# A decoder layer on one core: modulation weights on two of three parts of the first contraction, the final norm's weight ahead of r, and a turned order in the branches

## The chip, the cores and the metric

The kernel runs on one core of a Trainium2 chip. A core has TensorE (PE, matrix products into PSUM), VectorE (DVE), ScalarE (ACT), GpSimd (POOL), SyncE (SP, which here only issues DMAs) and 16 DMA engines that all queues share. The engines run on their own and wait for one another through semaphores; each takes its instructions in order. The metric is the device time of one execution in microseconds (us), lower is better.

## What is computed

One decoder layer on a sequence of 256 tokens of width 1024, in float32. A conditioning vector c gives nine modulation vectors, mod = silu(c) @ ada_w + ada_b; ada_w is 1024 x 9216, 36 MiB, and is read once.

```python
c_act = jax.nn.silu(c)
mod = c_act @ ada_w[l] + ada_b[l]
sh1, sc1, g1, sh2, sc2, g2, sh3, sc3, g3 = jnp.split(mod, N_MOD, axis=-1)
u = modulate(rms_norm(h, norm_ffn1_w[l]), sh1, sc1)
h = h + FFN_RESIDUAL_WEIGHT * g1[:, None, :] * swiglu(u, ffn1_w_in[l], ffn1_w_out[l])
u = modulate(rms_norm(h, norm_mix_w[l]), sh2, sc2)
h = h + g2[:, None, :] * hybrid_mixer(u, positions, mix_w_in[l], ...)
u = modulate(rms_norm(h, norm_ffn2_w[l]), sh3, sc3)
h = h + FFN_RESIDUAL_WEIGHT * g3[:, None, :] * swiglu(u, ffn2_w_in[l], ffn2_w_out[l])
return rms_norm(h, norm_final_w)
```

`rms_norm(x, w)` is x / sqrt(mean(x^2) + 1e-6) * w, `modulate(x, shift, scale)` is x * (1 + scale) + shift. `swiglu` multiplies by w_in (1024 x 5632), takes silu(gate) * up and multiplies by w_out (2816 x 1024). The mixer is one wide product u @ mix_w_in, an SSD (state space) branch and a retention branch, each multiplied by a matrix of 2048 x 1024, gated, added and multiplied by mix_w_out.

## The kernel before

Activations lie transposed: 128 features on the partitions, 256 tokens along the row, eight such tiles for the width of 1024. Every large product is made of three matmuls per pair of tiles (`mm3`): weights and activations are each split into a high half, rounded to the matmul's type (fp32r), and a low half, the remainder. high x high, high x low and low x high are added up in PSUM. For the weights the high half is a cast on ACT (`half`, L137), the low half a subtraction on DVE (L138). A group of 24 matmuls (8 row tiles x 3) fills one column tile of 128. `mm3` has a `turned` form that takes a triple in the order low x high, high x high, high x low, and `contract` and `pair_project` use it for the fifth of eight triples.

**Weights** come in tiles of 128 x 2048 floats (1 MiB; 768 KiB for a last part of six row tiles) from four staging buffers (tag wst, `STAGE_BUFS`), loaded on SP by `load`, split by `half` in two steps of 128 x 1024 into four high and four low buffers (`HALF_BUFS`). A staging buffer is free again when DVE has done the second low half.

**Modulation** is computed in the gaps. `ada_piece` (through `ada_next`) takes one quarter of one of the nine vectors: it loads 1 MiB of ada_w into a staging buffer on SP, and DVE forms two dot products of 128 x 1024 with the activated c (`ada_dots`, L195). After a vector's fourth quarter its bias is added (L207). `ada_todo` lists the pieces in the order of vectors 2, 4, 3, 5, 7, 6, 8; `ada_next(3, 5)` takes the next only if it belongs to vector 3 or 5.

**The first contraction**, `contract("ffn1_w_out", 22, ...)`, goes over four pairs of column tiles (f2). For each it loads three parts of 8, 8 and 6 row tiles (k0), splits, multiplies both column tiles, and after each part calls `each()`, here `ada_next(3, 5)`. With the eight pieces of vectors 3 and 5 left at its start, the first eight of its twelve parts take one each, and the last four none. After a pair's last part `residual`'s `done` updates h, squares it for the next norm and splits the new activations. Then `modulated` runs: `early_project` multiplies by the first two tiles of mix_w_in before the norm's factor is known, while DVE and ACT work it out (`rstd`) and apply it (L265, L236, L237); the dt projection (L590, L591) is the first to need the result.

Which instruction comes when is set by a planner that orders each engine's instructions from the program's order and its own estimate of durations; the steps of the mixer stand in a list written by hand (`ORDER`). In it, `branch` multiplies by 512 rows of w_br_ssd or w_br_ret: 4 row tiles, pairs of column tiles, 24 matmuls for each f2.

**The end.** The last contraction, with ffn2_w_out, is the other way round: tokens on the partitions (two tiles, tt), columns in blocks of 512, 256 and 256. For each block and tt: t = ps * gb (L1013), hN += t (L1014), ACT squares hN and sums along the row (L1015), and, except for the last block, hN is multiplied by the final norm's weight wf (L1017). After the last block r = 1/sqrt(mean + eps) (L183, L1025); the middle 256 columns are multiplied by r (L1029 on ACT for tt = 0, L1031 on DVE for tt = 1), the last 256 by r and wf in one step (L1032), the first 512 by r on ACT (L1034); each half row block is stored by a DMA of its own (L1033 and L1035).

Of the kernel before, what the change touches and what calls it, by code (L numbers as in the profile page):

```python
# [12 lines left out]
F32 = mybir.dt.float32  # L13
# [5 lines left out]
P = 128  # L19
# [61 lines left out]
def layer(ctx: ExitStack, tc: tile.TileContext, a, out, packing):  # L81
# [130 lines left out]
    def ada_next(*which):  # L212
        if ada_todo and (not which or ada_todo[0][0] in which):
            ada_piece(*ada_todo.pop(0))
# [112 lines left out]

    def contract(w, nk, acts, done, each=lambda: None):
        for f2 in range(KD // 2):
            ps = [proj_ps(), proj_ps()]  # L330
            for k0 in range(0, nk, 8):
                kn = min(8, nk - k0)
                st = load(w, k0 * P, kn, f2 * 256, 256)
                for f in range(2):
# [4 lines left out]
                    if k0 + kn == nk:  # L339
                        done(f2 * 2 + f, ps[f][:, 0, :])  # L340
                each()

# [144 lines left out]
    with tc.tile_pool(name=nm("fp"), bufs=1, reuse_waits="tile") as fp:  # L487
# [41 lines left out]
        while ada_todo[0][0] in (2, 4):  # L529
            ada_next()  # L530
        am = scale_col(V_N2, 4)
        contract("ffn1_w_out", NF, lambda kt: (ah[:, kt, :], alo[:, kt, :]),
                 residual(2, 0.5, am, lambda f: nT[:, f, :], u, 3), lambda: ada_next(3, 5))
        first = modulated(lambda f: nT[:, f, :], u, 3, "mix_w_in", (C_Z, C_Z + 256))
    with tc.tile_pool(name="mx", bufs=1, reuse_waits="tile") as mx:
# [259 lines left out]
        def branch(n, w, g, q):  # L795
# [6 lines left out]
            for f2 in range(2):  # L802
                hv = half(st[:, :, f2 * 256:(f2 + 1) * 256])
                ps = proj_ps()
                for f in range(2):
                    for kt in range(4):
                        mm3(ps[:, f, :], at(hv, al, kt, slice(f * P, (f + 1) * P)),
                            at(hl, al, kt), kt == 0, kt == 3)
                r = dst[:, f2 * 2:f2 * 2 + 2, :]
# [140 lines left out]
    with tc.tile_pool(name=nm("fp"), bufs=1, reuse_waits="tile") as fp:  # L950
# [43 lines left out]
        for bi, (c0, n) in enumerate(blocks):  # L994
# [15 lines left out]
            for tt in range(2):  # L1010
                t = fp.tile([P, 512], F32, tag="t", name=nm("t"), bufs=2)[:, :n]
                o = hN[:, tt, cs_]
                dve.tensor_tensor(t, ps[tt], gb[:, cs_], ALU.mult)  # L1013
                dve.tensor_tensor(o, o, t, ALU.add)  # L1014
                act.activation(t, o, AF.Square, accum_out=ss[:, tt, bi:bi + 1])  # L1015
                if not final:
                    dve.tensor_tensor(o, o, wf[:, cs_], ALU.mult)  # L1017
                if bi == 1:
# [3 lines left out]
                if final:  # L1022
# [3 lines left out]
                    rows = slice(tt * P, (tt + 1) * P)  # L1026
                    lo_, mid = hN[:, tt, :512], hN[:, tt, 512:768]
                    if tt == 0:
                        act.activation(mid, mid, AF.Copy, scale=r)  # L1029
                    else:  # L1030
                        dve.tensor_scalar(mid, mid, r, None, ALU.mult)  # L1031
                    dve.scalar_tensor_tensor(o, o, r, wf[:, cs_], ALU.mult, ALU.mult)  # L1032
                    nc.sync.dma_start(out[rows, 512:], hN[:, tt, 512:])  # L1033
                    act.activation(lo_, lo_, AF.Copy, scale=r)  # L1034
                    (act if tt else nc.sync).dma_start(out[rows, :512], lo_)  # L1035

# [41 lines left out]
```

## Time and profile before

| | us |
|---|---|
| median of three runs | 840.45 |
| lowest, highest | 838.89, 840.82 |
| the profiled execution | 840.93 |
| its span in the profile | 838.9 |

Rows of the profile give start and duration in us, or for groups of instructions the count, the busy time with the mean of one in ns, and the idle time of that engine just before them with what ended it. Engines are PE (matmul), PEld (weight load), DVE, ACT, POOL and SP; a q behind the name is the engine's sequencer issuing a DMA. Names are those of the program: wst the staging buffers, wh and wl high and low halves of the weights, ah and al those of the swiglu's activations, uh and ul those of the normed input, s the mixer's slots. PE's matmuls are pipelined: each shows a latency of about 0.28 us for 256 columns, and what counts is the distance from one start to the next.

The stretches in order: to 137 us the first swiglu's w_in products, 137.0 to 199.6 the first contraction, to about 216 the hand-over to the mixer, to 622 the mixer and its two branches, to 647 the product with mix_w_out, to 770 the second swiglu's w_in, to 831.8 the last contraction, and then the end of the final norm and the stores.

### The profile page before, as it was taken

How to read it: one execution, taken by the hardware profiler on the slowest of the kernel's cores; microseconds unless marked ns; L12 is line 12 of the kernel's file. 1: busy time of each engine (PE TensorE's matmuls, PEld its weight loads, DVE VectorE, ACT ScalarE, POOL GpSimd, SP SyncE). 2: the span in 40 equal slices, each digit the busy share in tenths (PEclk: the TensorE clock that was granted, in tenths of full speed). 3: DMA queues.
4: the chain of work that ended last, by engine and by line, in shares of the span. 5: the costliest groups of instructions: out<-in, count | busy, mean ns of one | idle time of the engine just before them, and what ended most of it. 6: DMA issues, size and time to landing. Idle time of an engine off the chain costs nothing.

```text
span 838.9 us, 16219 instructions
## 1 busy us (share of the span) xinstructions
PE 823.0 (98%) x6734; PEld 795.6 (95%) x6734; DVE 665.4 (79%) x1002; ACT 516.6 (62%) x743; POOL 10.3 (1%) x21
## 2 busy tenths in 40 slices
PE   7999999999999999999999999999999999999996
PEld 6999999999999979899999999999999999999896
DVE  5999879797989978688898778987979985455463
ACT  6675544465798688766565569765658654545342
POOL 0000000000100010000000000000000000000000
PEclk9999999999999999999999999999999999999999
DMA  9988789994595555446657663554565695455521
GB/s 365 414 343 292 270 302 331 342 366 172 204 309 198 196 173 214 166 163 225 216 202 301 245 220 139 200 203 160 218 225 179 259 337 201 155 201 177 188 89 50
DMA packets 30587, 193.14 MB, mean 230 GB/s; under 512 B 3489, under 2 KB 4129, under 8 KB 10034
## 3 DMA queue, kind: packets, MB, share of 16 engines
q1 hardware_dynamic: 28656, 186.40, 60.5%
q0 software_dynamic: 1568, 5.28, 2.1%
q8 instruction: 52, 0.85, 0.4%
q10 hardware_dynamic: 290, 0.44, 0.1%
q14 instruction: 21, 0.17, 0.1%
HBM read 191.02 MB, written 1.08 MB: 229 GB/s over the span
## 4 chain that ended last, share of the span: by engine, by line
PE 63%; DVE 14%; DMA 8%; ACT 8%; issue 7%; DVEq 0%; ACTq 0%; POOLq 0%
PE proj L151 17%; PE proj L153 17%; PE proj L152 17%; DVE wl L138 5%; DMA wst<-in_ada_w_dram 4%; DVE wst L195 3%; ACT wh L137 2%; ACT m L726 1%; DMA m<-rows 1%; PE proj L147 1%; PE proj L149 1%; PE proj L148 1%; DVE ada L195 1%; DVE cv L565 1%; DMA wst<-in_ffn_w_out_dram 1%
## 5 line engine op out<-in xcount | busy, mean ns | idle before, releaser
L137 ACT CAST wh<-wst 128x1024 fp32r<-128x1024 f32 (+1 forms) x263 | 272.0, 1039 | 220.2 <-PE proj L152 122.0
L138 DVE TENSOR_TENSOR wl<-wst,wh 128x1024 fp32r<-128x1024 f32 (+1 forms) x263 | 316.4, 1209 | 112.1 <-ACT wh L137 111.3
L151 PE MATMUL proj<-uh,wh 128*128 128x256 f32 (+1 forms) x1160 | 322.3, 278 | 0.0
L152 PE MATMUL proj<-ul,wh 128*128 128x256 f32 (+1 forms) x1160 | 321.6, 277 | 0.1
L153 PE MATMUL proj<-uh,wl 128*128 128x256 f32 (+1 forms) x1160 | 320.9, 277 | 0.0
L152 PEld LDWEIGHTS proj<-ul,wh 128*128 128x128 f32 x1160 | 217.9, 188 | 0.9 <-DVE ul L431 0.3
L153 PEld LDWEIGHTS proj<-uh,wl 128*128 128x128 f32 x1160 | 217.8, 188 | 0.5 <-DVE wl L409 0.3
L151 PEld LDWEIGHTS proj<-uh,wh 128*128 128x128 f32 x1160 | 218.0, 188 | 0.3 <-ACT wh L137 0.2
L151 PE MATMUL proj<-s,wh 128*128 128x256 f32 x312 | 86.9, 280 | 1.1 <-ACT s L811 0.8
L153 PE MATMUL proj<-s,wl 128*128 128x256 f32 x312 | 86.2, 277 | 0.0
L152 PE MATMUL proj<-s,wh 128*128 128x256 f32 x312 | 86.2, 277 | 0.0
L195 DVE SCALAR_TENSOR_TENSOR wst<-wst,cb 128x1024 f32<-128x1024 f32 x56 | 67.0, 1221 | 9.4 <-DMA wst<-in_ada_w_dram 9.2
L151 PEld LDWEIGHTS proj<-s,wh 128*128 128x128 f32 x312 | 58.4, 188 | 2.2 <-ACT s L811 1.6
L152 PEld LDWEIGHTS proj<-s,wh 128*128 128x128 f32 x312 | 58.6, 188 | 0.0
L153 PEld LDWEIGHTS proj<-s,wl 128*128 128x128 f32 x312 | 58.6, 188 | 0.0
L153 PE MATMUL proj<-ah,wl 128*128 128x256 f32 x152 | 42.3, 278 | 1.2 <-DVE wl L138 1.1
L151 PE MATMUL proj<-ah,wh 128*128 128x256 f32 x152 | 42.1, 277 | 0.4 <-ACT wh L137 0.4
L152 PE MATMUL proj<-wl,ah 128*128 128x256 f32 (+1 forms) x132 | 42.0, 318 | 0.0
L151 PE MATMUL proj<-wh,ah 128*128 128x256 f32 (+1 forms) x132 | 42.0, 318 | 0.0
L153 PE MATMUL proj<-wh,al 128*128 128x256 f32 (+1 forms) x132 | 42.0, 318 | 0.0
L147 PE MATMUL proj<-uh,wl 128*128 128x256 f32 x152 | 42.0, 276 | 0.0
L148 PE MATMUL proj<-uh,wh 128*128 128x256 f32 x152 | 42.0, 276 | 0.0
(265 smaller groups left out, 1370.8 us busy)
## 6 DMA issues: line engine op xcount, KB each, us to landing
wst<-in_mix_w_in_dram SPq DMA_DIRECT2D x52, 1024.0 KB, 4.9
wst<-in_ffn_w_in_dram SPq DMA_DIRECT2D x43, 1024.0 KB, 6.3
wst<-in_ada_w_dram SPq DMA_DIRECT2D x28, 1024.0 KB, 6.1
wst<-in_ffn_w_out_dram SPq DMA_DIRECT2D x17, 1024.0 KB, 5.1
ada<-in_ada_w_dram SPq DMA_DIRECT2D x16, 512.0 KB, 12.6
wst<-in_w_br_ssd_dram SPq DMA_DIRECT2D x8, 1024.0 KB, 5.2
wst<-in_w_br_ret_dram SPq DMA_DIRECT2D x8, 1024.0 KB, 5.0
wst<-in_ffn_w_out_dram SPq DMA_DIRECT2D x6, 768.0 KB, 5.4
```

The source lines that it names most:

```text
L137: act.copy(hi, v)
L138: dve.tensor_tensor(lo, v, hi.bitcast(F32), ALU.subtract)
L147: pe.matmul(o, l[1], r[0], start=False, stop=False, skip_group_check=skip)
L148: pe.matmul(o, l[0], r[0], start=False, stop=False, skip_group_check=skip)
L149: pe.matmul(o, l[0], r[1], start=False, stop=False, skip_group_check=skip)
L151: pe.matmul(o, l[0], r[0], start=first, stop=False, skip_group_check=skip)
L152: pe.matmul(o, l[0], r[1], start=False, stop=False, skip_group_check=skip)
L153: pe.matmul(o, l[1], r[0], start=False, stop=last, skip_group_check=skip)
L195: dve.scalar_tensor_tensor(st[:, i, :], st[:, i, :], 1.0, cb, ALU.mult, ALU.mult, accum_out=raw[:, j, f0 + i:f0 + i + 1])
L565: dve.scalar_tensor_tensor(t[:, f, sh:], ps[:, f, :T - sh], wc(3 - sh), t[:, f, sh:], ALU.mult, ALU.add)
L726: act.activation(m[c][:, hl, :], m[c][:, hl, :], AF.Relu, bias=cs[:, c, hd:hd + 1], scale=-1.0)
```

## The change

1. `contract` has a new argument `rest`. With `rest=3`, used for ffn1_w_out alone, `each()` is left out after the parts whose running number, from 0, is a multiple of 3: the first part of each column pair. The eight pieces then fall on parts 2, 3, 5, 6, 8, 9, 11 and 12.
2. `branch` turns one triple of each group of 24: the third row tile of the second column tile.
3. In the final norm t takes the sum, ACT squares into a tile q of its own, and hN = t * wf for all three blocks. After r is known, tt = 0 is multiplied by r in one step of 1024 columns on ACT and stored by one DMA of 512 KB on SP; tt = 1 has 512 columns on DVE with a store on SP, and 512 on ACT with a store on ACT's queue.

```diff
-    def contract(w, nk, acts, done, each=lambda: None):
+    def contract(w, nk, acts, done, each=lambda: None, rest=0):
+        parts = (nk + 7) // 8
         for f2 in range(KD // 2):
...
-                each()
+                if not rest or (f2 * parts + k0 // 8) % rest:
+                    each()
...
         contract("ffn1_w_out", NF, lambda kt: (ah[:, kt, :], alo[:, kt, :]),
-                 residual(2, 0.5, am, lambda f: nT[:, f, :], u, 3), lambda: ada_next(3, 5))
+                 residual(2, 0.5, am, lambda f: nT[:, f, :], u, 3), lambda: ada_next(3, 5), 3)
...
                         mm3(ps[:, f, :], at(hv, al, kt, slice(f * P, (f + 1) * P)),
-                            at(hl, al, kt), kt == 0, kt == 3)
+                            at(hl, al, kt), kt == 0, kt == 3, turned=f == 1 and kt == 2)
...
                 dve.tensor_tensor(t, ps[tt], gb[:, cs_], ALU.mult)
-                dve.tensor_tensor(o, o, t, ALU.add)
-                act.activation(t, o, AF.Square, accum_out=ss[:, tt, bi:bi + 1])
-                if not final:
-                    dve.tensor_tensor(o, o, wf[:, cs_], ALU.mult)
+                dve.tensor_tensor(t, o, t, ALU.add)
+                q = fp.tile([P, 512], F32, tag="q", name=nm("q"), bufs=1)[:, :n]
+                act.activation(q, t, AF.Square, accum_out=ss[:, tt, bi:bi + 1])
+                dve.tensor_tensor(o, t, wf[:, cs_], ALU.mult)
...
-                    lo_, mid = hN[:, tt, :512], hN[:, tt, 512:768]
+                    lo_, up = hN[:, tt, :512], hN[:, tt, 512:]
                     if tt == 0:
-                        act.activation(mid, mid, AF.Copy, scale=r)
+                        act.activation(hN[:, 0, :], hN[:, 0, :], AF.Copy, scale=r)
+                        nc.sync.dma_start(out[rows, :], hN[:, 0, :])
                     else:
-                        dve.tensor_scalar(mid, mid, r, None, ALU.mult)
-                    dve.scalar_tensor_tensor(o, o, r, wf[:, cs_], ALU.mult, ALU.mult)
-                    nc.sync.dma_start(out[rows, 512:], hN[:, tt, 512:])
-                    act.activation(lo_, lo_, AF.Copy, scale=r)
-                    (act if tt else nc.sync).dma_start(out[rows, :512], lo_)
+                        dve.tensor_scalar(up, up, r, None, ALU.mult)
+                        nc.sync.dma_start(out[rows, 512:], up)
+                        act.activation(lo_, lo_, AF.Copy, scale=r)
+                        act.dma_start(out[rows, :512], lo_)
```

## The prediction, made before the change was run

> **What bounds the kernel now.** I read the page first: busy times, the slices, then the chain.
>
> ```profile
> span 838.9 us, 16219 instructions
> PE 823.0 (98%) x6734; PEld 795.6 (95%) x6734; DVE 665.4 (79%) x1002; ACT 516.6 (62%) x743; POOL 10.3 (1%) x21
> ...
> PE   7999999999999999999999999999999999999996
> ...
> DMA  9988789994595555446657663554565695455521
> ```
>
> TensorE is busy 98% of the span; only the two ends show a slice below 9. No engine but PE can shorten this kernel by being faster; an edit pays only where PE starts its matmuls later than it could. So I looked at PE's spacing, stretch by stretch (columns: window, length, then PE, PEld, DVE, ACT and POOL busy with counts, granted clock, DMA share, GB/s).
>
> ```profile
> 137.00:199.61 62.61, 60.97 (x529) 60.18 (x528) 51.60 (x78) 30.96 (x47) 0.00 (x0) 1.00 0.84 308
> 443.50:492.40 48.90, 48.90 (x434) 48.90 (x433) 38.93 (x49) 26.95 (x34) 0.00 (x0) 1.00 0.70 265
> 334.22:339.93 5.71, 5.71 (x51) 5.71 (x50) 4.26 (x7) 2.52 (x6) 1.23 (x2) 1.00 0.77 306
> 600.00:605.40 5.40, 5.40 (x50) 5.40 (x49) 5.14 (x9) 3.05 (x5) 0.00 (x0) 1.00 0.69 256
> ```
>
> Counts include two matmuls that a window's edges cut. The second row is an undisturbed stretch: 48.90 us for 432 starts, 0.1132 us each, at a granted clock of 1.00. The first row is the contraction with ffn1_w_out: 22 row tiles x 8 column tiles x 3 = 528 matmuls, at 0.1132 us 59.8 us; it took 62.6. **2.8 us are lost there**, and this is the stretch that the first edit touches. Who was late is in the grouped instructions of that stretch (last column: idle before, and its releaser):
>
> ```profile
> L151 PE MATMUL proj<-ah,wh 128*128 128x256 f32 x152 | 42.1, 277 | 0.4 <-ACT wh L137 0.4
> L153 PE MATMUL proj<-ah,wl 128*128 128x256 f32 x151 | 42.0, 278 | 1.2 <-DVE wl L138 1.1
> ...
> L138 DVE TENSOR_TENSOR wl<-wst,wh 128x1024 fp32r<-128x1024 f32 (+1 forms) x26 | 29.2, 1140 | 10.1 <-ACT wh L137 9.9
> ...
> L137 ACT CAST wh<-wst 128x1024 fp32r<-128x1024 f32 (+1 forms) x24 | 22.8, 976 | 25.9 <-DMA wst<-in_ffn_w_out_dram 17.8 <-PE proj L152 5.9 <-DVE h L321 2.2
> L195 DVE SCALAR_TENSOR_TENSOR wst<-wst,cb 128x1024 f32<-128x1024 f32 x14 | 16.7, 1222 | 0.8 <-DMA wst<-in_ada_w_dram 0.7
> ...
> L321 DVE SCALAR_TENSOR_TENSOR h<-proj,g,h 128x256 f32<-128x256 f32 x7 | 3.3, 478 | 0.0
> L325 DVE TENSOR_TENSOR ul<-nT,uh 128x256 fp32r<-128x256 f32 x6 | 2.5, 420 | 0.1
> ```
>
> PE waits for the low halves (DVE), these for the high halves (ACT), these for the weights' DMA, 17.8 us in all. Two resources feed this stretch, DMA and DVE. DMA, over 137 to 168 us, and one of its late landings:
>
> ```profile
> GB/s 315 143 341 349 381 312 370 285 328 349 317 159 222 285 433 412 349 317 412 433 423 423 423 291 328 373 275 330 309 420 285 307 285 243 180 211 275 402 423 433
> DMA packets 1474, 10.19 MB, mean 329 GB/s; under 512 B 168, under 2 KB 168, under 8 KB 424
> ```
> ```profile
> 159.00 0.33 SPq L116 DMA_DIRECT2D wst<-in_ffn_w_out_dram  x1
> ...
> 181.37 37.07 SPq L116 DMA_DIRECT2D wst<-in_mix_w_in_dram  x9
> ```
> ```profile
> 166.83 2.00 ACT L137 CAST wh<-wst 128x1024 fp32r<-128x1024 f32 x2 [5.09 <-DMA wst<-in_ffn_w_out_dram]
> ```
>
> The tile issued at 159.00 could be cast only at 166.83: 7.8 us for 1 MiB, because a 1 MiB modulation tile shares the queue with each weight tile. A full part is 48 matmuls, 5.4 us of PE; it draws 2 MiB, 2.10 MB, at 329 GB/s 6.4 us. DMA loses 1 us a part as long as each part has its modulation tile.
>
> DVE in the same stretch and behind it (window, length, busy and count, clock, DMA share, GB/s):
>
> ```profile
> 168.00:184.00 16.00, 15.95 (x25) 1.00 0.96 358
> 184.00:199.60 15.60, 9.66 (x14) 1.00 0.55 215
> 199.60:216.00 16.40, 15.57 (x40) 1.00 0.54 193
> ```
>
> DVE is full until 184 us and idle for 5.9 us of the next 15.6, with DMA at 0.55: the eight modulation pieces are crammed into the first eight of twelve parts.
>
> **The change part by part.** *Modulation on two of three parts.* Nothing is removed or added: eight pieces, each one DMA of 1 MiB on SP and two dot products on DVE (L195, 2 x 1.22 us, 2.4). They move from parts 1 to 8 to parts 2, 3, 5, 6, 8, 9, 11, 12. A column pair (three parts, 132 matmuls, 14.9 us of PE) drew 2.75 MiB of weights and 3 MiB of modulation, 6.03 MB: at 329 GB/s 18.3 us. It will draw 4.75 MiB, 4.98 MB: 15.1 us. With the lead that the queue has at 137 us I take DMA as no longer late. DVE's work for a pair, from the means above: six low halves at 1.14, 6.8; three residual steps for each of two tiles (L321 0.48, L325 0.42, and the sum of squares, of L325's shape), 2.6; dots 3 x 2.4 = 7.2 before, 4.8 after: 16.6 before against 14.9 of PE, 14.2 after. Both overloads go; the last pair, with 5.9 us of DVE idle, gets two pieces (4.8 us) that it did not have. At best the 2.8 us go whole; at worst nothing does. I take **-2.3 us**, because DVE is then at 95% throughout and an unlucky order of dots before a low half still costs a few tenths.
>
> The Trainium skill (DMA: Bandwidth & Descriptors, Specifications) gives a fabric ceiling of 435 GB/s; by it a part's 2.10 MB would take an estimated 4.8 us, less than PE's 5.4, and bytes would not be the bound. Single slices here do reach 433, but the mean over 31 us is 329; by the page alone the gain would be that of the third rival below.
>
> What is next late: the last piece now sits behind part 12, at the hand-over to the early projection of mix_w_in, and stands on SP ahead of that projection's two tiles. Before, these were issued from 181.37 us on, far ahead of their use at 199.7. Four staging buffers go round, so now they wait for those of part 11 and of the seventh piece. How far DVE runs ahead of PE decides:
>
> ```profile
> 174.04 2.36 DVE L138 TENSOR_TENSOR wl<-wst,wh 128x1024 fp32r<-128x1024 f32 x2
> ...
> 187.36 1.22 DVE L138 TENSOR_TENSOR wl<-wst,wh 128x1024 fp32r<-128x1024 f32 x1
> ```
>
> The second row is part 11's last low half, done at 188.6; PE comes to that half 2.7 + 4.1 = 6.8 us ahead of the hand-over, at 192.9, so the lead is 4.3 us. The first row, part 8 in the crammed stretch, has none: PE waited for it at 175. With 4.3 the tiles would be issued 11.1 us ahead of use; they need at most 7.8 to land and 2.1 (means of L137 and L138) to be split: enough by 1.2. And DVE's stretch behind the hand-over has 0.83 us free of 16.40; a piece that slips in costs up to 2.4 - 0.8 = 1.6 us. I take **+0.3 us** for both, range 0 to 4.7.
>
> *Turned order in the branches.* No instruction is added; three matmuls of 24 in each of 32 groups swap places. One stretch of branch work runs at 5.71/48 = 0.119 us a matmul, another at 5.40/48 = 0.1125. In the undisturbed stretch above (432 matmuls, with turned triples every 24) the spacing is already 0.113, so turning costs nothing there; that bounds the loss at 0. If it brings the slow stretch to 0.113 from the triple on, 30 matmuls x 0.006 = 0.2 us. I take **-0.1**, between the two.
>
> [...]
>
> *The final norm.* This is the tail, where PE is done and every step is on the path.
>
> ```profile
> 831.49 0.28 PE L153 MATMUL proj<-wh,al 128*128 128x256 f32 x1
> ```
> ```profile
> 831.50 0.16 DVE L1025 RECIPROCAL ss<-ss 128x1 f32<-128x1 f32 x1 [0.96 <-ACT ss L183]
> 831.70 0.48 DVE L1032 SCALAR_TENSOR_TENSOR hN<-hN,ss,wf 128x256 f32<-128x256 f32 x1
> 832.10 0.42 DVE L1013 TENSOR_TENSOR t<-proj,gb 128x256 f32<-128x256 f32 x1
> 832.55 0.43 DVE L1014 TENSOR_TENSOR hN<-hN,t 128x256 f32<-128x256 f32 x1
> ...
> 834.08 0.35 DVE L1031 TENSOR_SCALAR hN<-hN,ss 128x256 f32<-128x256 f32 x1
> 834.35 0.48 DVE L1032 SCALAR_TENSOR_TENSOR hN<-hN,ss,wf 128x256 f32<-128x256 f32 x1
> ```
> ```profile
> 831.70 0.51 ACT L1029 ACTIVATE hN<-hN,ss 128x256 f32<-128x256 f32 x1 [0.23 <-DVE ss L1025]
> 832.11 0.71 ACT L1034 ACTIVATE hN<-hN,ss 128x512 f32<-128x512 f32 x1
> 833.01 0.42 ACT L1015 ACTIVATE t<-hN 128x256 f32<-128x256 f32 x1 [0.20 <-DVE hN L1014]
> ...
> 834.08 0.72 ACT L1034 ACTIVATE hN<-hN,ss 128x512 f32<-128x512 f32 x1 [0.23 <-DVE ss L1025]
> 834.83 0.39 ACTq L1035 DMA_DIRECT2D out_dram<-hN  x1
> ```
> ```profile
> out_dram<-hN SPq DMA_DIRECT2D x3, 256.0 KB, 2.1
> ...
> out_dram<-hN ACTq DMA_DIRECT2D x1, 256.0 KB, 2.7
> ```
>
> PE's last matmul ends at 831.77, but DVE takes the second half's product only at 832.10, behind L1032 of the first half. L1032 goes; the added multiplication by wf (one 128x256 tensor_tensor, 0.42 us) runs while ACT squares (into a tile of its own, q, since t is still read), in both halves, and DVE has nothing else there. So the product starts at about 831.81, the sum ends at 832.70. ACT then holds it: its one copy of 128x1024 from 831.70 costs 0.71 plus two steps of 0.20 (what 512 costs over 256), 1.11 us, to 832.8; the square starts at about 832.85 against 833.01. From there the chain is the same to ACT's copy of 512 and its store: issued at about 834.67 against 834.83, **-0.16 us**. DVE's product of 512 columns costs 0.35 plus at most as much again, 0.70 us from 833.92, 834.6: not later than ACT. The first half's one store of 512 KB starts at 832.8; at twice the 2.1 us of 256 KB it lands at 837.0, before the second half's (834.67 + 2.7 = 837.4), though they share engines for 2 us. Bounds: -0.3 (DVE's lead passed on in full) to +0.7 (a third of a 256 KB store's time lost to sharing).
>
> **The sum**: -2.3 + 0.3 - 0.1 - 0.16 = -2.3 us (rounded). Against the profiled execution's own 840.93 us (span 838.9 and 2.0 around it) that is 838.6; that run lies 0.5 above the median of the three, 840.45, so against the median **838.2**.
>
> **The rivals.** (1) *The stall moves to the hand-over.* The last piece's dots fall into DVE's full stretch at 199.6 to 216: -2.3 + 1.6 - 0.26 = -1.0, **839.5**. For it: 0.83 us free there. Against: the piece's tile waits only for part 10's buffer and should land before PE is through part 11, and DVE had 5.9 us idle just there. (2) *Slower: the early projection's two tiles come late.* If DVE's lead over PE is used up, so that part 11's buffer comes free only when PE starts its second half, 6.8 us ahead of the hand-over, then 7.8 to land and 2.1 to split make PE wait 3.1 us; the dots' 1.6 come on top; against a gain of 2.8 and 0.26: +1.6, **842.1**. It decides from a lead under 3.1 us; 4.3 in the relaxed stretch is not far from that, but a wait of the full size needs no lead at all, as at 175 us. (3) *The change does not do what it says*: slices at 433 GB/s mean that the four staging buffers, not bytes, hold the loads back; then spacing them leaves most of the stall: -0.7 for it, -0.26 for the rest, **839.5**. Against: 0.96 DMA share in the stretch.
>
> **How the numbers follow.** Forecast (837.2 to 838.7) 0.54; better still 0.03; rival 1 0.21; rival 3 0.14; rival 2 0.08, most of it short of full size. The range must leave out two tenths at most: from 836.9 to 840.4. A measurement of this kernel tells about 0.2% (1.7 us) from no change. Faster by more, below 838.8: 0.57. Within: rivals 1 and 3 and a weak rival 2, 0.37. Slower: 0.06.
>
> **What would show it.** The contraction's 528 matmuls should span 60 us, with no idle time of L151 or L153 behind wh or wl and ACT's wait for ffn1_w_out's DMA well under 17.8 us; DVE's busy share should be even over its four pairs. The first matmul of the early projection should follow the last of the contraction within 0.2 us, and the stretch to the dt projection should stay near 16.4 us; a wait for mix_w_in's DMA there is rival 2, dots behind 197 us are rival 1. In the tail, the second half's product should start within 0.1 us of PE's end and the last store be issued 3.2 us behind PE's last start instead of 3.34. The forecast is wrong if the contraction still takes over 62 us, or if what it saves is seen again ahead of the dt projection.

## The result, and where the time went

The changed kernel takes **847.02 us** (median; 843.25 to 848.4), the kernel before, on the same chip, 839.59 (838.16 to 840.82): ratio 1.0078, 95% interval 1.0063 to 1.0094, by that ratio some 6.5 us slower. The prediction was 838.2, with 0.06 for slower. The profiled execution of the changed kernel took 845.92 us, its span is 844.1 against 838.9.

To place the 5.2 us I set landmarks of PE's timeline side by side, instructions that both traces show by name, since some matmul records are missing and counting would drift:

| stretch of PE | before, us | after, us | after minus before |
|---|---|---|---|
| to the contraction's first start | 137.01 | 136.85 | -0.2 |
| contraction, to the first start behind it | 62.73 | 61.44 | -1.3 |
| hand-over, from there to the first projection behind L601 (after: L603) | 15.50 | 19.84 | +4.3 |
| from there to the first branch product (334.22, 336.66) | 118.98 | 118.53 | -0.5 |
| from there to the branch product that waits (341.80, 345.92) | 7.58 | 9.26 | +1.7 |
| the next 30 us, to the next product of s and st | 29.96 | 31.55 | +1.6 |
| from there to PE's last start | 459.73 | 459.77 | 0.0 |
| from PE's last start to the end of the span | 7.41 | 6.86 | -0.55 |

In this pair of traces the contraction gained and the tail gained; two places lost more: the hand-over to the early projection, which the prediction had named and priced at 0.3, and a wait at 342 us.

The windows of the changed kernel that answer to those of the prediction, and one more (columns as there: window, length, PE, PEld, DVE, ACT, POOL busy with counts, granted clock, DMA share, GB/s):

```profile
137.00:199.61 62.61, 61.64 (x537) 60.95 (x535) 49.96 (x77) 29.68 (x44) 0.00 (x0) 1.00 0.81 300
168.00:184.00 16.00, 15.55 (x137) 15.36 (x136) 13.19 (x21) 7.89 (x12) 0.00 (x0) 1.00 0.84 306
184.00:199.60 15.60, 15.09 (x129) 14.59 (x127) 12.88 (x22) 7.54 (x12) 0.00 (x0) 1.00 0.74 282
199.60:216.00 16.40, 14.23 (x100) 13.27 (x101) 14.97 (x36) 10.72 (x22) 0.00 (x0) 0.90 0.48 175
202.00:206.00 4.00, 3.49 (x12) 2.77 (x13) 2.92 (x6) 2.94 (x6) 0.00 (x0) 0.57 0.73 274
```

The load is spread as intended: DVE in the second and third row is busy 13.2 and 12.9 us, where it was 15.95 and 9.66, and the DMA share falls from 0.96 to 0.84 and rises from 0.55 to 0.74. The price is in the last two: behind the contraction PE starts 100 matmuls where it started 133, and between 202 and 206 us only 12, at a granted clock of 0.57. In the trace of before no window ahead of the tail shows a clock under 0.97.

**The chain behind it.** First SP's queue, at which the early projection's two tiles are asked for (before: 181.37 and 183.71):

```profile
177.98 0.33 SPq L116 DMA_DIRECT2D wst<-in_ada_w_dram  x1
178.85 0.33 SPq L116 DMA_DIRECT2D wst<-in_ffn_w_out_dram  x1
181.41 0.33 SPq L116 DMA_DIRECT2D wst<-in_ada_w_dram  x1
...
189.66 0.33 SPq L116 DMA_DIRECT2D wst<-in_mix_w_in_dram  x1
...
191.50 0.33 SPq L116 DMA_DIRECT2D wst<-in_mix_w_in_dram  x1
```

SP then issues nothing for eight microseconds: all four staging buffers are held. Who holds them stands in DVE's timeline (start, duration, line, operation, count, in brackets the wait ahead of it):

```profile
184.67 1.23 DVE L195 SCALAR_TENSOR_TENSOR wst<-wst,cb 128x1024 f32<-128x1024 f32 x1 [3.29 <-DMA wst<-in_ada_w_dram]
...
186.21 1.21 DVE L138 TENSOR_TENSOR wl<-wst,wh 128x1024 fp32r<-128x1024 f32 x1
...
188.41 1.21 DVE L195 SCALAR_TENSOR_TENSOR wst<-wst,cb 128x1024 f32<-128x1024 f32 x1
...
190.22 2.08 DVE L138 TENSOR_TENSOR wl<-wst,wh 128x1024 fp32r<-128x1024 f32 x2
...
199.03 1.23 DVE L138 TENSOR_TENSOR wl<-wst,wh 128x1024 fp32r<-128x1024 f32 x1 [1.99 <-ACT wh L137]
200.17 0.48 DVE L321 SCALAR_TENSOR_TENSOR h<-proj,g,h 128x256 f32<-128x256 f32 x1
200.57 1.22 DVE L138 TENSOR_TENSOR wl<-wst,wh 128x1024 fp32r<-128x1024 f32 x1
201.70 0.42 DVE L250 TENSOR_TENSOR ssum<-ssum,sq 128x256 f32<-128x256 f32 x1
```

DVE stands 3.29 us before part 11's modulation tile, asked for at 177.98, and part 11's low halves are queued behind. Its second dot product ends at 189.6, and at 189.66 the first tile of mix_w_in is asked for; the second of part 11's low halves (the first of the two at 190.22, with one of part 12) ends at about 191.4, and at 191.50 follows the second tile. ACT shows when they have landed, and PE what waited for them:

```profile
194.59 1.05 ACT L137 CAST wh<-wst 128x1024 fp32r<-128x1024 f32 x1 [3.38 <-DMA wst<-in_mix_w_in_dram]
197.95 2.00 ACT L137 CAST wh<-wst 128x1024 fp32r<-128x1024 f32 x2 [2.31 <-DMA wst<-in_mix_w_in_dram]
```
```profile
200.31 0.39 PE L153 MATMUL misc<-uh,wl 128*128 128x258 f32 x1 [0.76 <-DVE wl L138]
...
202.17 0.84 PE L219 MATMUL misc<-ssum,k 128*128 128x256 f32 x2 [1.12 <-DVE ssum L250]
203.35 1.22 PE L219 MATMUL misc<-sq,k 128*128 128x256 f32 x2 [0.34 <-ACT sq L248]
...
204.80 0.42 PE L153 MATMUL proj<-uh,wl 128*128 128x258 f32 x1
205.01 0.42 PE L151 MATMUL proj<-uh,wh 128*128 128x258 f32 x1
```

The second tile lands 6.4 us after its request, 0.3 ahead of the hand-over at 198.29, and still has to be split. Then DVE's order makes it worse: the low half at 199.03 waits 1.99 us for that tile's high half, and behind it stands L321, the residual of the last column tiles, and with it the norm's sums (L250), for which PE waits at 202.17. After that PE runs at half speed until about 206: the last two rows are 0.21 us apart, where such matmuls of 258 columns start every 0.12 us in the trace of before.

**The wait at 342** is on the ACT copy L813, in line behind an activation (L728; L726 in the kernel before) that waits for a DMA issued by POOL (ACT's row before, then after; then PE after):

```profile
339.05 1.28 ACT L726 ACTIVATE m<-m,cs 128x128 f32<-128x128 f32 x4 [3.19 <-DMA m<-rows]
```
```profile
343.18 1.28 ACT L728 ACTIVATE m<-m,cs 128x128 f32<-128x128 f32 x4 [4.87 <-DMA m<-rows]
```
```profile
345.92 0.57 PE L151 MATMUL proj<-s,wh 128*128 128x256 f32 x1 [2.55 <-ACT s L813]
```

The DMA landed 7.6 us after its issue, in the trace of before 6.0, and then the clock went to half from 346 to 350, the 1.6 us of the table's next row. I do not count this to the change, though no run settles it. Over all traces of this study ACT's wait is 3.1 to 3.6 us in thirteen and 4.1 to 4.9 in five (the changed kernel, e5, e7, e10, e15). Two of the five, e7 and e15, lose nothing at the hand-over, and e1, which loses 4.6 there, waits 3.34; yet three of the four traces whose hand-over takes 19 us or more have the long wait, and only two of the other fourteen. The requests beside this DMA do not tell the cases apart: in the traces of before, of the changed kernel and of e14 SP asks for weight tiles 5.1 and 0.2 us ahead of it, and it lands after 6.0, 7.6 and 6.4 us.

### The profile page after: what moved, and what is told of

It reads as the page before. It is cut to its first block, busy times and chain, and to the rows that moved or that the text cites. A ratio compares the mean times of both kernels' runs of the same rounds, so it can differ in the third digit from the quotient of the medians.

```text
span 844.1 us, 16214 instructions
## 1 busy us (share of the span) xinstructions
PE 826.1 (98%) x6734; PEld 799.2 (95%) x6734; DVE 666.1 (79%) x1002; ACT 517.1 (61%) x742; POOL 10.3 (1%) x21
## 4 chain that ended last, share of the span: by engine, by line
PE 77%; DVE 8%; DMA 7%; issue 5%; ACT 3%; DVEq 0%; ACTq 0%; SPq 0%; POOLq 0%
PE proj L151 21%; PE proj L153 21%; PE proj L152 21%; DMA wst<-in_ada_w_dram 4%; DVE wl L138 3%; PE proj L148 2%; PE proj L147 2%; PE proj L149 2%; DVE wst L195 2%; PE misc L151 1%; PE misc L152 1%; PE misc L153 1%; ACT wh L137 1%; DMA m<-rows 1%; DMA k<-in_consts_dram 1%
## 5 line engine op out<-in xcount | busy, mean ns | idle before, releaser
L151 PE MATMUL proj<-s,wh 128*128 128x256 f32 x280 | 78.8, 283 | 2.9 <-ACT s L813 2.6
L153 PE MATMUL proj<-s,wl 128*128 128x256 f32 x280 | 78.0, 279 | 0.0
L152 PE MATMUL proj<-s,wh 128*128 128x256 f32 x280 | 78.0, 279 | 0.0
L151 PEld LDWEIGHTS proj<-s,wh 128*128 128x128 f32 x280 | 53.2, 191 | 4.0 <-ACT s L813 3.4
L152 PEld LDWEIGHTS proj<-s,wh 128*128 128x128 f32 x280 | 53.4, 191 | 0.0
L153 PEld LDWEIGHTS proj<-s,wl 128*128 128x128 f32 x280 | 53.3, 190 | 0.0
L152 PE MATMUL proj<-al,wh 128*128 128x256 f32 x152 | 42.0, 276 | 0.0
```

Source lines behind the costliest of these rows:

```text
L151: pe.matmul(o, l[0], r[0], start=first, stop=False, skip_group_check=skip)
L152: pe.matmul(o, l[0], r[1], start=False, stop=False, skip_group_check=skip)
L153: pe.matmul(o, l[1], r[0], start=False, stop=last, skip_group_check=skip)
```

## The experiments

All ratios are against the kernel before on the same chip, run beside the kernel in question. "Contraction" and "hand-over" are the stretches of the table above, from each kernel's profiled execution; "half clock" names the stretches ahead of the tail with a granted clock under 0.97.

| | what | us | ratio, 95% interval | contraction | hand-over | half clock at |
|---|---|---|---|---|---|---|
| before | | 839.6 to 840.2 | 1 | 62.73 | 15.50 | none |
| after | all three edits | 847.02 | 1.0078 (1.0063, 1.0094) | 61.44 | 19.84 | 202, 346 |
| e1 | edit 1 alone | 849.12 | 1.0095 (1.0068, 1.0123) | 63.22 | 20.08 | 204 |
| e2 | edits 2 and 3 | 839.70 | 0.9998 (0.9987, 1.0009) | 63.75 | 15.49 | none |
| e3 | edit 3 alone | 839.88 | 0.9994 (0.9981, 1.0008) | 61.83 | 15.50 | none |
| e4 | pieces off the last two parts | 839.1 | 0.9991 (0.998, 1.0002) | 61.23 | 15.95 | none |
| e5 | PE kept busy in the hand-over | 847.61 | 1.0093 (1.007, 1.0117) | 65.25 | 19.01 | 158, 348 |
| e6 | dots of 16 columns | 837.15 | 0.9966 (0.9954, 0.9977) | 59.84 | 15.50 | none |
| e7 | dots without tiles | 840.43 | 0.9997 (0.9981, 1.0012) | 60.10 | 15.49 | none |
| e8 | vector 5 in the mixer's last places | 846.43 | 1.0077 (1.0055, 1.0099) | 61.39 | 15.50 | 622 |
| e9 | vector 5 in new places | 841.58 | 1.0025 (1.0008, 1.0041) | 60.30 | 15.49 | none |
| e10 | dots one piece later | 845.99 | 1.0059 (1.0036, 1.0081) | 62.34 | 20.19 | 202, 346 |
| e11 | one dot of two on POOL and ACT | 852.93 | 1.014 (1.0118, 1.0163) | 74.60 | 17.29 | 180 |
| e12 | e11 on e4's parts | 852.3 | 1.0138 (1.012, 1.0156) | 74.33 | 15.50 | 176, 196 |
| e13 | part 12's piece moved | 838.9 | 0.9983 (0.9971, 0.9995) | 60.65 | 16.34 | none |
| e14 | part 11's piece moved | 838.58 | 0.998 (0.9968, 0.9993) | 61.11 | 15.51 | none |
| e15 | seven pieces, one in the mixer | 841.36 | 1.0013 (0.9998, 1.0029) | 61.08 | 15.49 | none |
| e16 | six pieces, two in the mixer | 840.83 | 1.0014 (0.9997, 1.0031) | 60.72 | 15.50 | none |

**e1, e2, e3: the edits one by one.** e1 is the first hunk of the diff alone, e3 the last alone, e2 leaves only the argument `3` of `contract` out.

> The first edit alone (modulation on two of three parts; branches and final norm as before). Theory A (the loss is made at the hand-over by this edit: the early projection's two mix_w_in tiles come late, DVE is held behind them, and PE's idle time halves the granted clock afterwards): 844 to 849 us, 0.6 to 1.0% slower, a granted clock below 0.5 to 1.0 in a stretch near 204 us and the contraction itself some 1.5 us shorter. Theory B (the loss comes from another edit, the branches' order or the added tile q): 837 to 839 us, as forecast for this edit.

> The second and third edit without the first. Theory A: 839.0 to 839.5 us, 0.03 to 0.1% faster than before (tail -0.2 to -0.6, branches 0 to -0.2), no stretch with a clock at a half. Theory B: 844 us or more.

> The third edit alone. By the prediction's tail -0.16 us, by the profile of the changed kernel up to -0.6 us: 839.0 to 839.5. If the branches' turned order is worth anything, this run lies above the run of both edits by up to 0.2 us; that is below what the rounds can tell.

The loss is edit 1's: all three times lie 0.1 to 0.4 us above the ranges given, and those of e1 and e2 far from theory B's. What e1 does not show is the gain in the contraction that its expectation named: 63.22 us, where the kernel before takes 62.73. The turned order can't be told from nothing: e2 and e3, which differ in it alone, have overlapping intervals, and the stretch from 372 us to PE's last start, with most of the branches, takes 459.85 us with it and 459.69 without. The tail's gain is seen in the trace (below), not in the times.

**e4: the same edit, with the last two parts free.** Pieces on parts 1, 2, 4, 5, 7, 8, 9 and 10:

```diff
-                if not rest or (f2 * parts + k0 // 8) % rest:
+                if f2 * parts + k0 // 8 not in rest:
...
-                 residual(2, 0.5, am, lambda f: nT[:, f, :], u, 3), lambda: ada_next(3, 5), 3)
+                 residual(2, 0.5, am, lambda f: nT[:, f, :], u, 3), lambda: ada_next(3, 5), (2, 5, 10, 11))
```

> All three edits, but the eight modulation pieces on parts 1, 2, 4, 5, 7, 8, 9 and 10: spaced like the change at first, none on the last two parts. Theory A: the contraction keeps 1 to 2 us of what it gained, the early projection's tiles are issued at least 4 us ahead of those in the changed kernel, no half clock at 204 us: 837 to 839 us. Theory C (spacing itself lets DVE's lead run out, wherever the pieces stand): still above 842.

The hand-over is all but whole again (15.95), and no half clock appears. So not the spreading costs, but where the last pieces fall.

**e5: is it the clock?** Six matmuls of 128 x 128 on constants ahead of the norm's mean:

```diff
-        ps = early_project(w, cols, u, 1, lambda: rs.append(rstd(sums, mean_m)))
+        def between():
+            if n:
+                warm(n)
+            rs.append(rstd(sums, mean_m))
+        ps = early_project(w, cols, u, 1, between)
```

> The changed kernel with six matmuls of ones (128x128, result not read) put in front of the norm's mean at the first hand-over, where PE waits. Theory A2 (part of the loss is the granted clock, halved because PE stood idle): no slices at a half near 204 us, 844 to 845.5 us, 1.5 to 3 below the changed kernel. Theory A1 (only the waits themselves cost): 846.5 to 848, the same as the changed kernel or up to 0.5 above.

In this trace the contraction ends later, at 202.25 us; the stretch from there on runs at a clock of 1.00:

```profile
202.00:216.00 14.00, 12.49 (x98) 11.61 (x97) 11.94 (x26) 10.02 (x19) 0.00 (x0) 1.00 0.54 205
```

The hand-over takes 19.01 us, six more matmuls included, against 19.84, 20.08 and 20.19 in the changed kernel, e1 and e10. So by this one trace the half clock is worth about 1 us of the loss there (the window above would give (1 - 0.57) x 4 = 1.7 at most), and the other 3 are waiting. The time, 847.61, lies in the range of A1 all the same: its executions differ by more than 1 us (844.64 to 849.82), and the contraction of the profiled one had a stretch at half clock of its own (158 to 162).

**e6, e7: DVE's time, or the tiles?** e6 loads the tiles but multiplies only 16 columns of each; e7 makes the same dot products on a tile that is in SBUF already and loads none.

```diff
-        ada_dots(ada_rows(stage(), j, 2 * k2), j, 2 * k2)
+        if j in (3, 5):
+            st = ada_rows(stage(), j, 2 * k2)
+            for i in range(2):
+                dve.scalar_tensor_tensor(st[:, i, :16], st[:, i, :16], 1.0, cb[:, :16], ALU.mult,
+                                         ALU.mult, accum_out=raw[:, j, 2 * k2 + i:2 * k2 + i + 1])
...
```

> The changed kernel with the dot products of vectors 3 and 5 over 16 columns instead of 1024: the modulation tiles are loaded and hold their buffers as before, DVE's 1.2 us each are gone (most of those two vectors' modulation is left out). If DVE's time is what makes the hand-over late: 837 to 839 us. If DVE waits for the tile's DMA in front of part 11's low halves and the buffers come free too late: 843 to 847, with DVE's wait for a modulation tile of 3 us still there.

> The changed kernel with the dot products of vectors 3 and 5 on data that is already in SBUF: DVE has the same instructions, but the eight modulation tiles are not loaded and take no staging buffer (those vectors' modulation is wrong). If the DMA and the buffers make the hand-over late: 835 to 838 us, early projection's tiles issued 8 us or more ahead of use. If DVE's time does: 843 to 847.

e6 leaves out most of the sums of vectors 3 and 5, e7 the whole of their weights. Either one clears the hand-over. In e6 the tiles of mix_w_in are asked for at 181.63 and 185.49, although DVE waits for modulation tiles more than in the changed kernel, 10.5 us against 8.3. A wait of DVE for a tile thus costs nothing here by itself; it hurts together with the dots' own time. Both also bring the contraction to 59.84 and 60.10 us, the 59.8 of PE's own spacing: with either load gone it loses nothing. The time of e7, 840.43, is still no shorter than before, and above the 835 to 838 that I expected: its profiled execution, one of the fastest with 838.32, has the long wait at 342 (1.75 us on PE), and what the slower ones lose no trace shows.

**e8, e9: vector 5 out of the contraction.** e8 gives vector 5 to the mixer's twelve "ada" places, so that vectors 7 and 6 move back and the last four places, empty before, are filled. e9 leaves these empty and adds four places (after v.4, z.2.1, v.7 and z.3.1).

```diff
-                 residual(2, 0.5, am, lambda f: nT[:, f, :], u, 3), lambda: ada_next(3, 5), 3)
+                 residual(2, 0.5, am, lambda f: nT[:, f, :], u, 3), lambda: ada_next(3), 3)
...
-            "rs": ret_scores, "rv": ret_values, "rn": ret_norm, "ada": lambda: ada_next(7, 6),
+            "rs": ret_scores, "rv": ret_values, "rn": ret_norm, "ada": lambda: ada_next(5, 7, 6),
```

> The changed kernel with only vector 3 in the contraction (four pieces, on parts 2, 3, 5 and 6) and vector 5 ahead of 7 and 6 in the mixer's twelve places for a piece, of which four found none before. By theory A the hand-over is clear of pieces and the contraction loses under 1 us: 836.5 to 838.5. If the mixer has no room for four more MiB and 10 us of DVE behind its steps: 840 or more.

The first hand-over is clean, and the loss appears at the next one, ahead of mix_w_out, where the last pieces now lie (windows, then ACT, then PE, of e8):

```profile
600.00:620.00 20.00, 20.00 (x179) 20.00 (x178) 20.00 (x35) 5.83 (x9) 0.00 (x0) 1.00 0.89 336
622.00:630.00 8.00, 4.50 (x20) 4.05 (x21) 7.71 (x10) 5.90 (x10) 0.00 (x0) 0.58 0.45 166
```
```profile
619.61 1.99 ACT L137 CAST wh<-wst 128x1024 fp32r<-128x1024 f32 x2 [8.28 <-DMA wst<-in_mix_w_out_dram]
```
```profile
626.51 0.58 PE L151 MATMUL proj<-s,wh 128*128 128x256 f32 x1 [3.11 <-ACT wh L137]
```

DVE is full for 20 us (18.0 in the trace of before), the first tile of the next matrix is asked for at 612.39 us (before: 602.67), ACT waits 8.28 us for it, PE waits, the clock falls: the same picture 420 us later. So it is not something of this contraction alone: two hand-overs show the loss, each when pieces stand just ahead of it.

> All three edits, but no modulation piece stands in front of a hand-over: vector 3's four pieces follow parts 2, 4, 6 and 8 of the contraction, vector 5's four go into the mixer at four new places (after v.4, z.2.1, v.7 and z.3.1), so that vectors 7 and 6 keep their places and the last four places stay empty as before. Theory A (a piece placed in the last parts ahead of a hand-over makes DVE wait and holds the next weights' tiles back): no wait at 200 to 205, none at 620 to 630, no window at half clock; 836.5 to 838.5 if the mixer takes four pieces for nothing, as DVE has idle time there. Rival B (the mixer is as full as the contraction, a piece costs the same wherever it is put): 840 or more, with new waits of PE at the four places. Under B part of the run's gain in the contraction, about 1.5 us, would still show at 198.

Theory A held for the places (no wait at 200 or 622, no half clock) and failed for the time: 841.58, B's "840 or more". The gain in the contraction is there, 2.4 us, and 0.9 of it is lost again between the hand-over and the first branch product. That is the trace of one of the faster executions (839.8); what the slower ones, up to 845.76, lose on top is not shown.

**e10: an edit that did nothing.** The tile is loaded at its part and its dots are called one piece later.

```diff
+        if old:
+            ada_dots(*old)
...
-                 residual(2, 0.5, am, lambda f: nT[:, f, :], u, 3), lambda: ada_next(3, 5), 3)
+                 residual(2, 0.5, am, lambda f: nT[:, f, :], u, 3), lambda: ada_late(3, 5), 3)
+        ada_late()
```

> The changed kernel, with each piece's tile loaded at its part as there, but its two dot products issued one of the piece's turns later (the last pair behind the contraction's end). Theory A1 (DVE, which works in order, stands waiting for a modulation tile that has only just been asked for, with part 11's low halves behind it): DVE's waits for modulation tiles fall from 8.3 us to under 2, the low halves of part 11 come earlier, the hand-over loses 1 to 2 us in place of 4.8: 838 to 843. Rival A2 (the staging buffers are what counts: a tile that stays in its buffer longer holds the next weights back): the weight tiles are asked for later than in the changed kernel and the time is 846 or more, with DVE's waits for modulation tiles gone all the same.

The time looks like A2's, but it isn't evidence for it: DVE still waits 9.4 us for modulation tiles, and from 137 to 206 us DVE's instructions stand in the same order in both traces, dots included. The planner put them back. The run is a repeat of the changed kernel (845.99, hand-over 20.19 us) and tells nothing of A1.

**e11, e12: one dot product of two away from DVE**, as a product on POOL and a sum on ACT, on the changed kernel's parts and on e4's.

```diff
+            if i and j in (3, 5):
+                nc.gpsimd.tensor_tensor(st[:, i, :], st[:, i, :], cb, ALU.mult)
+                act.activation(st[:, i, :], st[:, i, :], AF.Copy,
+                               accum_out=raw[:, j, f0 + i:f0 + i + 1])
+                continue
```

> The changed kernel with the same pieces at the same places, but of the two dot products of a piece only one on DVE; the other is a product on POOL (10 us busy in the whole span) and a sum on ACT (idle for half of the contraction). DVE is so rid of 8 x 1.22 = 9.8 us in the contraction, 1.2 us of it in each of the last two parts, and the whole computation stays. Theory A (the dots that come in the last parts use up DVE's lead, so buffers come free late): the early projection's tiles are asked for at 182 to 186 us in place of 189.7 and 191.5, the hand-over loses under 1 us, 837 to 840. Rival B (a modulation tile holds its staging buffer at least as long, since POOL's product and ACT's sum follow each other, and ACT stands in line for POOL with the high halves behind it): tiles asked for at 189 or later, 845 or more. No row here has a product of this size on POOL; above about 4 us for one I would expect B.

> As the one before (one dot product of each piece on POOL and ACT), with the pieces on parts 1, 2, 4, 5, 7, 8, 9 and 10, which leaves the last two parts free as in the run that gave 839.1. If DVE's time is what was left to win in the contraction, its gain of about 2 us comes without a loss at the hand-over: 836.5 to 838.5, faster than both kernels. If POOL's product disturbs DVE or holds buffers, the stalls of the contraction stay or grow: 839 or more.

Both are far slower. B's line of ACT behind POOL is there: 31.3 us of waiting (sum from 137 to 215 in e11). What B did not have is that a product on POOL, 2.4 to 3.4 us and so under my bound of 4, holds up DVE: low halves that meet it take nearly three times as long (POOL, then DVE, of e11):

```profile
157.41 3.37 POOL L196 TENSOR_TENSOR wst<-wst,cb 128x1024 f32<-128x1024 f32 x1 [9.14 <-DMA wst<-in_ada_w_dram]
```
```profile
157.35 1.23 DVE L200 SCALAR_TENSOR_TENSOR wst<-wst,cb 128x1024 f32<-128x1024 f32 x1 [3.37 <-DMA wst<-in_ada_w_dram]
...
158.50 3.37 DVE L138 TENSOR_TENSOR wl<-wst,wh 128x1024 fp32r<-128x1024 f32 x1
```

In e11 PE waits 10.3 us for low halves in that stretch. The runs say nothing of the theory that they were made for.

**e13, e14: one of the two late pieces moved.** Pieces on parts 1, 2, 3, 5, 6, 8, 9 and 11, or the same with 12 in place of 11; the edit is e4's with other numbers.

> All edits, the last piece alone moved away from part 12: pieces on parts 1, 2, 3, 5, 6, 8, 9 and 11. In the trace of the changed kernel the early projection's first tile was asked for at 189.66 us, the moment that the dots of part 11's piece ended, and its second at 191.50, when part 11's last low half ended. Theory A-buffers (four buffers go round, and each piece in the last two parts pushes both tiles one buffer later): without part 12's piece the first tile is asked for at 180 to 183, the second at 187 to 190, the hand-over loses under 1 us, no half clock: 838 to 840.5. Rival A-order (DVE stands before part 11's modulation tile with low halves and residual steps behind it, so the hand-over is late whatever the buffers do): the loss stays at 2 us or more, 842 or more.

> The counterpart: part 11's piece moved away and part 12's kept, pieces on parts 1, 2, 3, 5, 6, 8, 9 and 12. A-buffers: the tiles still wait for one buffer more than before, but DVE, without the dots and the wait in front of part 11's low halves, frees them sooner: asked for at 184 to 188 and 187 to 190, a loss of 0 to 2 us, 838 to 842. A-order: DVE's wait falls on part 12's low halves or on the early projection's instead, the loss is 2 us or more, 842 or more.

Both come out as the buffers have it, and both are a little faster than the kernel before. SP's queue, e13 and then e14:

```profile
182.60 0.33 SPq L116 DMA_DIRECT2D wst<-in_mix_w_in_dram  x1
...
189.96 0.33 SPq L116 DMA_DIRECT2D wst<-in_mix_w_in_dram  x1
```
```profile
183.58 0.33 SPq L116 DMA_DIRECT2D wst<-in_mix_w_in_dram  x1
...
187.42 0.33 SPq L116 DMA_DIRECT2D wst<-in_mix_w_in_dram  x1
```

In e13 DVE still stands 2.4 us before part 11's tile, and the second tile of mix_w_in is asked for only at 189.96, 7.6 us ahead of that kernel's hand-over at 197.58; the hand-over loses 0.8 us. With both pieces it is 191.50, 6.8 us ahead, and the loss 4.3. I read the step as steep because the first tile is late as well then, because DVE's order hangs the norm's sums behind the second, and because the clock goes last; no run takes these three apart, except that e5 puts the clock at about 1 us.

**e15, e16: seven or six pieces in the contraction, the rest in the mixer** (e9's new places, the first one or two).

> All edits, seven pieces in the contraction (parts 1, 2, 4, 5, 7, 8, 10), and vector 5's last in the mixer at one new place after v.4, so that its other places and the four empty ones stay as they are. One piece less is 2.4 us of DVE and 1 MiB. If the contraction's lack was DVE and DMA together, its gain of 1.5 to 2.5 us comes without a loss at the hand-over and the mixer takes one piece for nothing: 837.5 to 839.5. If a piece in the mixer costs its 2.4 us there as it did in the contraction: 839.5 to 841.5.

> All edits, six pieces in the contraction (parts 1, 3, 5, 6, 8 and 9) and two in the mixer, after v.4 and after z.2.1. The same two answers with two pieces: 837 to 839 if the mixer has room for them, as its DVE does by the page; if it hasn't, as the run with four pieces there (841.58) hints, 840 or more.

The second answer in both, though neither can be told from the kernel before. Their contractions and hand-overs are as good as e14's, so the mixer does not take the pieces for nothing. From the hand-over to the first branch product all three kernels with new places take 119.8 or 119.9 us, against 118.4 to 119.4 in all others, and PE has a wait there (1.0 to 1.2 us) that no other trace has. Of e16:

```profile
317.12 1.10 PE L708 MATMUL misc<-xe,bn 128*128 128x512 f32 x2 [1.02 <-DVE xe L699]
```

Why DVE is late there I have not followed; in e15 the long wait at 342 comes on top.

## Why the prediction was wrong

**The step that failed is the hand-over**, "I take +0.3 us for both, range 0 to 4.7". It cost 4.3 in the trace, close to the end that I had kept for the range and then cut off by giving rival 2 a chance of 0.08. The mechanism was named correctly in rival 2, down to the buffers ("those of part 11 and of the seventh piece"; the rows show both, 189.66 and 191.50). What was wrong is the lead. I read 4.3 us of it from the trace of before, where part 11's last low half ends at 188.6 and PE comes to it at 192.9. But in that trace no dots lie in the last four parts. The change puts two pieces there, 4.8 us of DVE, as the paragraph on DVE says itself, and they come with tiles for which DVE must wait (3.29 us in one row). In the changed kernel that low half ends at about 191.4, and PE is already there and waits for it:

```profile
191.50 0.38 PE L153 MATMUL proj<-ah,wl 128*128 128x256 f32 x1 [0.46 <-DVE wl L138]
```

That is **no lead at all, not 4.3 us**; rival 2 applies from a lead under 3.1, and its condition, a buffer that comes free only when PE starts on part 11's second half, is met to the letter. I measured the slack with the old load and spent it with the new one.

**Rival 2 was right in kind and too cheap.** It had 842.1: 3.1 for the wait and 1.6 for the dots. Those 4.7 are near the 4.3 that the hand-over lost, but by other terms: the second tile landed in 6.4 us, not 7.8; about 3 us are PE's waits, for the low half and then for the norm's sums behind it in DVE's order, and about 1 is the clock at half, which the prediction did not have. Most of what is left to the profiled execution's 845.92 is the smaller gain in the contraction and the 3.3 us at 342.

**The contraction, -2.3,** is the second step that failed. It is -1.3 in the pair of profiles, and even that is not secure. Traces with the old arrangement have 62.73 (before), 63.75 (e2) and 61.83 (e3); those with the change's own have 61.44 (after), 62.34 (e10), 63.22 (e1) and 65.25 (e5, with its half clock). The two sets overlap, so for the change as it was made no gain is shown. Pieces placed otherwise come out lower: e4, e13 and e14 have 61.23, 60.65 and 61.11, below all three of the old arrangement. What was wrong is "I take DMA as no longer late": ACT's wait for ffn1_w_out's DMA is down from 17.8 us to 8.0, but DVE's wait for modulation tiles is up from 0.7 to 8.3, and DVE, which I put at 95%, is busy for 49.96 us of 62.61 (groups of the changed kernel, 137.00 to 199.61, last column):

```profile
L137 ACT CAST wh<-wst 128x1024 fp32r<-128x1024 f32 (+1 forms) x24 | 22.8, 974 | 19.2 <-DMA wst<-in_ffn_w_out_dram 8.0 <-DMA wst<-in_mix_w_in_dram 5.7 <-PE proj L152 5.6
```
```profile
L195 DVE SCALAR_TENSOR_TENSOR wst<-wst,cb 128x1024 f32<-128x1024 f32 x15 | 18.1, 1220 | 8.3 <-DMA wst<-in_ada_w_dram 8.3
```

Rival 3 (most of the stall stays, -0.7) is thus not refuted for the change itself; for e4, e13 and e14, 1.5 to 2.1 under the 62.73 of before, it looks too small. Its cause, the buffers in place of the bytes, no run tests alone. With the hand-over out of the way the sum comes near: e14, which differs from the changed kernel only in that part 1 has a piece and part 11 has none, takes 838.58, by its ratio 1.7 us less than the kernel before, and e13 838.9, 1.4 less; the forecast was 2.3 less. That is another kernel than the one forecast, and does not make the forecast right.

**Turned order, -0.1.** Not to be told from zero, by e2 and e3. **The tail, -0.16.** The steps came as described, with a larger gain (the changed kernel's tail, ACT, and PE's last start):

```profile
837.24 0.28 PE L153 MATMUL proj<-wh,al 128*128 128x256 f32 x1
```
```profile
837.44 1.15 ACT L1031 ACTIVATE hN<-hN,ss 128x1024 f32<-128x1024 f32 x1 [0.23 <-DVE ss L1027]
838.50 0.40 ACT L1018 ACTIVATE q<-t 128x256 f32<-128x256 f32 x1
...
840.30 0.35 ACTq L1037 DMA_DIRECT2D out_dram<-hN  x1
```

From PE's last start to the last store's issue it is 3.06 us, against 3.34 before and 3.18 predicted; ACT's copy took 1.15, for 1.11 predicted, and as foreseen the square follows it at once. From the store to the end of the span it is 3.8 us against 4.1. In all -0.55, the same within 0.05 in e2, e3 and e14.

## What to carry to other kernels

Slack read in a trace is slack under the load of that trace: before work is moved into it, subtract the moved work, its own wait for its data included, and see what stands in order behind it. Filler work (here modulation pieces) should end a few buffers ahead of a change of matrix, because the next matrix's first tiles wait for the same ring of buffers. Here one piece in the last two parts cost 0.8 us at the hand-over (e13) or nothing (e14), and two cost 4.3. The medians of e13 and e14 and of the changed kernel lie some 8 us apart; part of that is the wait at 342 (3.3 us in the profiled execution), which is not tied to the two pieces. And compare orders before reading a time: an edit of the program's order need not reach the engines.

## What the hardware showed that I had not expected

PE's clock halves after short waits. In the hand-over of the changed kernel no wait is over 1.12 us, yet 202 to 206 us ran at 0.57. In the mixer waits of 2.55 (after), 2.27 (e5) and 2.04 us (e10) at 342 were followed by half clock, and 2.40 (e15) and 1.75 (e7) were not, so the length alone doesn't decide. Each of the three lost 1.5 to 1.6 us in the 30 us that follow (31.55, 31.45 and 31.52 against 29.9 to 30.0 in all other traces). The Trainium skill (TensorE: Matmul & The Clock Gate, Part 1: The HAM clock gate) has the drop come after at least one idle window of about 3.4 us, in windows that run free of the kernel. Free windows would fit the mixed outcomes; a whole idle window does not fit these rows.

A product on POOL and an instruction on DVE can hold each other up, and the one that starts first goes on at its own pace. In the rows of e11 above the dot product starts 0.06 us ahead of POOL's product and takes 1.23 us, as always; the low half starts under it, takes 3.37 in place of 1.22 and ends 1.1 us behind POOL's, almost a whole length of its own. Where a dot product starts behind POOL, it fares like the low half (POOL, then DVE, of e12):

```profile
134.64 2.77 POOL L196 TENSOR_TENSOR wst<-wst,cb 128x1024 f32<-128x1024 f32 x1 [134.19 <-DMA wst<-in_ada_w_dram]
```
```profile
135.07 3.42 DVE L200 SCALAR_TENSOR_TENSOR wst<-wst,cb 128x1024 f32<-128x1024 f32 x1
```

It ends 1.1 us behind POOL. POOL's product in turn takes 2.4 us where no such DVE row overlaps its start (139.56 in e12), and 3.3 to 3.4 where a dot product has just started. The Trainium skill (GPSIMD Engine Reference, 1. Specifications) says that GpSimd shares its SBUF interfaces with VectorE, with contention for DVE instructions that have two SBUF inputs; the rows agree, for the subtraction and for the dot product, which both have two (3.37 and 3.42 us).
